# Jensen-Shannon divergence on one core: row groups in six rotating buffers, other column ranges, and the last row group closed on ScalarE

## The chip, the core and the metric

The kernel runs on one core of a Trainium2 chip. The time is the device time of one execution in microseconds (us), lower is better. The core's engines work side by side, each through its own instructions in order: TensorE (PE) multiplies matrices into PSUM, VectorE (DVE) does elementwise arithmetic and reductions, ScalarE (ACT) evaluates functions such as the logarithm, GpSimd (POOL) here only issues loads, SyncE (SP) issues loads and the store. Sixteen DMA engines move the data.

## The reference

```python
# p, q: (1024, 4096) fp32, each row sums to 1
m = 0.5 * (p + q)
kl_pm = np.sum(p * np.log(p / (m + 1e-8) + 1e-8), axis=-1)
kl_qm = np.sum(q * np.log(q / (m + 1e-8) + 1e-8), axis=-1)
return (0.5 * (kl_pm + kl_qm)).astype(np.float32)   # (1024,)
```

The kernel takes a logarithm of p, of q and of p+q for every column, so three logs for each column of a row: with a = ln p, b = ln q and c = ln((p+q)/2), the result is half the sum of p(a-c) + q(b-c). All three logs carry the same scale inside, which cancels.

## The kernel before

The 1024 rows are eight row groups of 128 rows, one row per partition, with 4096 columns each. Every row group is cut into column ranges, by four tables that need not agree: LOADS (what one DMA brings), LOGS (what one ScalarE instruction takes of p and q), SUMS (what PE adds up to p+q in one PSUM tile, and what one log of the sum takes), PRODUCTS (the width of a tile that holds the logs of p and q).

All input is loaded once. The first two ranges of row group 0 come as fp32 over the SyncE and ScalarE queues (lines 169 to 172). All others come through POOL's queue (lines 179 and 180, `cast_loads`), which casts fp32 to fp16 on the way: p and q of each range, 27 instructions each. Before the change every row group has an SBUF tile of its own (`data`, lines 155 to 158), so no load waits for a tile; all are issued in the order of the table.

The operations have one-letter names, with the number of their range:

- `a`: VectorE adds p and q of a range that came as fp32 (line 240). `F`: PE adds p and q of any other range by multiplying both with the identity into one PSUM tile, 512 columns at a time, p then q (line 265). Two PSUM tiles take turns.
- `p`, `q`: ScalarE logs p, then q, of one range of LOGS; from range SPLIT on, one instruction takes both (`q`, line 281). `c`: ScalarE logs a sum (line 299). There are C_BUFS tiles for c.
- `u`, `x` (row groups 0 to 5): VectorE subtracts c from both logs (line 311), then multiplies by p and q (line 321). `X`: PE adds the products up into the row group's PSUM accumulator of 256 columns (line 360, 256 columns a matmul).
- `m`, `s`, `M`, `S` (row groups 6 and 7, from APART on): the products p ln p, q ln q (line 328) and (p+q) c (line 339) are formed apart, which needs no subtraction, and PE adds them up with weights 0.5 and -0.5. The last FUSED_M of the m and the last FUSED_S of the s (lines 332 and 343) multiply and reduce in one VectorE instruction, into a running sum `run`.
- `f`: VectorE folds a row group's accumulator into one column of the result (line 382, or line 385 with the running sum). In the last row group ScalarE folds (`A`, line 371, Copy with an accumulated output) and VectorE adds the running sum (`f7`, line 376).
- `W`: PE multiplies without effect, to stay busy (line 253).

The order of each engine's operations is written out by hand in PE_ORDER, ACT_ORDER and DVE_ORDER. A loop at the end of the kernel emits them so that each operation comes after those it needs (`after`), without changing the order on an engine. The store of the result (line 470) is last.

The end of the three orders before:

```python
# ScalarE: ... c29 q27 q28 c30 q29 c31 q30 q31 q32 A7
# VectorE: ... s30 m26 s31 m27 m28 m29 f7
# TensorE: ... F30 F31 M24 M25 W10 M26 W4 M27 M28
```

Of the kernel before, what the change touches and what calls it, by code (L numbers as in the profile page):

```python
# [13 lines left out]
AW = 256  # L14
AB_BUFS = 5
C_BUFS = 4

LOADS = [  # L20
    [512, 256, 832, 960, 768, 768],
    [512, 896, 832, 768, 1088],
    [1280, 1408, 1408],
    [1152, 1408, 1536],
    [1280, 1536, 1280],
    [1408, 1408, 1280],
    [256, 1536, 1536, 768],
    [2048, 2048],
]
LOGS = [  # L30
    [512, 256, 832, 960, 768, 768],
    [512, 896, 832, 768, 1088],
    [1280, 1408, 1408],
    [1152, 1408, 1536],
    [1280, 1536, 1280],
    [1408, 1408, 1280],
    [256, 1536, 1536, 768],
    [768, 1024, 896, 512, 512, 384],
]
PRODUCTS = [  # L40
    [512, 256, 832, 1728, 768],
    [512, 896, 832, 1856],
    [1280, 1408, 1408],
    [1152, 1408, 1536],
    [1280, 1536, 1280],
    [1408, 1408, 1280],
    [1792, 1536, 768],
    [768, 1024, 896, 512, 512, 384],
]
SUMS = [  # L50
    [512, 256, 448, 384, 384, 384, 960, 768],
    [512, 896, 832, 768, 1088],
    [1280, 1408, 1408],
    [1152, 1408, 1536],
    [1280, 1536, 1280],
    [1408, 1408, 1280],
    [256, 1536, 1280, 1024],
    [1536, 1408, 1152],
]
HW = 2  # L60
SPLIT = 5

APART = 6
FUSED_M = 1
FUSED_S = 4

# [6 lines left out]
ACT_ORDER = """  # L73
p0 q0 c0 p1 q1 c1 p2 q2 c2 c3 p3 q3 c4 c5 p4 q4 c6 q5 c7 q6 c8 q7 c9 q8 c10 q9 c11 q10 c12
q11 c13 q12 c14 q13 c15 q14 c16 q15 c17 q16 c18 c19 q17 q18 c20 c21 q19 c22 q20 c23 q21
c24 c25 q22 c26 q23 q24 c27 q25 c28 q26 c29 q27 q28 c30 q29 c31 q30 q31 q32 A7
"""
PE_ORDER = """
W22 F2 F3 X0 X1 F4 F5 X2 X3 F6 X4 X5 F7 F8 X6 F9 X7 F10 X8 F11 X9 F12 X10 X11 F13 W8 X12
F14 F15 X13 F16 X14 F17 X15 F18 X16 F19 X17 F20 X18 F21 X19 F22 X20 F23 X21 F24 F25 X22  # L80
F26 S25 X23 F27 F28 S26 X24 M21 F29 S27 M22 M23 F30 F31 M24 M25 W10 M26 W4 M27 M28
"""
DVE_ORDER = """
a0 a1 u0 x0 u1 x1 u2 u3 x2 x3 u4 u5 x4 x5 u6 x6 u7 x7 u8 x8 f0 u9 x9 u10 x10 u11 x11 u12
x12 u13 f1 x13 u14 x14 u15 x15 u16 x16 f2 u17 x17 u18 x18 u19 x19 f3 u20 x20 u21 x21 u22
f4 x22 u23 s25 x23 u24 s26 x24 m21 s27 f5 m22 s28 m23 s29 m24 f6 m25 s30 m26 s31 m27 m28
m29 f7
"""
# [3 lines left out]
def kernel(  # L92
# [46 lines left out]

    small = ctx.enter_context(tc.tile_pool(name="small", bufs=1))  # L140
    lnp = ctx.enter_context(tc.tile_pool(name="lnp", bufs=AB_BUFS))
    mid = ctx.enter_context(tc.tile_pool(name="mid", bufs=C_BUFS))
# [9 lines left out]
    for i in range(HW):  # L152
        t32 = small.tile([P, 2, loads[i][2]], fp32, tag=f"pq32_{i}")
        early.append(t32)
    data = []
    for g in range(n_rg):
        t16 = small.tile([P, 2, n_cols - (split if g == 0 else 0)], fp16, tag=f"pq{g}")
        data.append(t16)

    def pq(g, c0, w):  # L160
        if g == 0:
            for i in range(HW):
                if loads[i] == (g, c0, w):
                    return early[i]
            c0 -= split
            assert c0 >= 0
        return data[g][:, :, c0 : c0 + w]
# [7 lines left out]
    nc.scalar.activation(out=warm, in_=warm, func=Act.Ln)  # L175
    def cast_loads(some):
        for g, c0, w in some:
            v = pq(g, c0, w)
            nc.gpsimd.dma_start(out=v[:, 0, :], in_=pv[g, :, c0 : c0 + w])  # L179
            nc.gpsimd.dma_start(out=v[:, 1, :], in_=qv[g, :, c0 : c0 + w])  # L180

    cast_loads(loads[HW : HW + 1])
    ident = small.tile([P, P], fp16, tag="ident")
# [4 lines left out]
    nc.vector.memset(zero, 0.0)  # L188
    cast_loads(loads[HW + 1 :])
    half = small.tile([P, P], fp16, tag="half")  # L190
# [24 lines left out]
    for g in range(n_rg):  # L215
        own = [o for o in dve_order if o == ("f", g) or (fused(*o) and range_of(*o)[0] == g)]
        if g < n_rg - 1 or act_folds:
            own = [o for o in own if o[0] != "f"] + [("f", g)]
        chain[g] = own
# [4 lines left out]
    def next_run(o, g):  # L224
        before = state["last"].get(g, 0.0)
        if o == chain[g][-1]:
            return before, res[:, g : g + 1]
        k = state["used"]
        state["used"] += 1
        state["last"][g] = run[:, k : k + 1]  # L230
        return before, run[:, k : k + 1]
# [92 lines left out]
    def op_m(k):  # L324
        g, c0, w = prods[k]
        u = pq(g, c0, w)
        if not fused("m", k):
            nc.vector.tensor_tensor(out=ab[k], in0=u, in1=ab[k], op=Alu.mult)  # L328
            product["M", k] = ab[k]
            return  # L330
        before, now = next_run(("m", k), g)
        nc.vector.tensor_tensor_reduce(
            out=ab[k], in0=u, in1=ab[k], scale=0.5, scalar=before,
            op0=Alu.mult, op1=Alu.add, accum_out=now,
        )

    def op_s(j):
        if not fused("s", j):
            nc.vector.tensor_tensor(out=c[j], in0=s[j], in1=c[j], op=Alu.mult)  # L339
            product["S", j] = c[j].unsqueeze(1)  # L340
            return
        before, now = next_run(("s", j), parts[j][0])
        nc.vector.tensor_tensor_reduce(  # L343
            out=c[j], in0=s[j], in1=c[j], scale=-0.5, scalar=before,
            op0=Alu.mult, op1=Alu.add, accum_out=now,
        )

    def add_up(kind, i):
# [9 lines left out]
        for n, (t, b) in enumerate(todo):  # L358
# [7 lines left out]
            )  # L366

    def op_A(g):
        folded = small.tile([P, 1], fp32, tag="folded")
        unused = small.tile([P, AW], fp16, tag="unused")  # L370
        nc.scalar.activation(out=unused, in_=acc[g][:, :AW], func=Act.Copy, accum_out=folded)  # L371
        state["folded"] = folded

    def op_f(g):
        if act_folds and g == n_rg - 1:
            nc.vector.tensor_tensor(
                out=res[:, g : g + 1], in0=state["folded"], in1=state["last"][g], op=Alu.add
            )
            return
        before, now = next_run(("f", g), g)  # L380
# [24 lines left out]
    def after(kind, i):  # L405
# [21 lines left out]
        if kind == "f":  # L427
            if act_folds and i == n_rg - 1:
                return chain[i][:-1] + [("A", i)]
            return chain[i][: chain[i].index(("f", i))] + adds[i]  # L430
        if kind == "A":
            return adds[i]
        return []

    accumulator(0)
    ops = dict(a=op_a, F=op_F, p=op_p, q=op_q, c=op_c, u=op_u, x=op_x, m=op_m, s=op_s, f=op_f, A=op_A)
    queues = [list(pe_order), list(act_order), list(dve_order)]
    emitted = set()
# [25 lines left out]
    if act_folds:  # L464
        want.add(("A", n_rg - 1))
    assert emitted == want
    pe_order = [o for o in pe_order if o[0] != "W"]
# [33 lines left out]
```

## Time and profile before

| | |
|---|---|
| median of 4 runs | 98.15 us (97.92 to 98.23) |
| profiled execution, its own time | 98.23 us |
| its span (first to last instruction) | 96.4 us |
| granted TensorE clock, mean | 0.982 |
| PE / DVE / ACT / POOL busy, share of the span | 74% / 85% / 93% / 30% |
| read from HBM | 33.55 MB, 348 GB/s over the span |

The profile is one execution. An engine's busy time is the time in which it worked on instructions; the span is cut into 40 equal slices of 2.41 us, and a digit gives the busy share of a slice in tenths. A wait is idle time of an engine, put down to whatever released it last. The chain that ended last is followed back from the last instruction, at each step to what released it. A row of the timeline has the start in us, the duration in us, the engine, the line, the operation, the output and inputs with their sizes, and in brackets the idle time just before it and who ended it. The trace also holds when each of the sixteen parts of a load landed; a load counts as landed with the last of them.

### The profile page before, as it was taken

What the parts mean: (1) busy time and instruction counts of PE and PEld (TensorE: products, weight loads), DVE (VectorE), ACT (ScalarE), POOL (GpSimd) and SP (SyncE); (2) the same over time, 40 slices, a digit from 0 to 9 for tenths busy, and PEclk for the clock granted to TensorE, in tenths of its full rate; (3) what the DMA queues carried; (4) which work ended last, traced back from release to release, by engine and by line L of the source; (5) the groups of instructions that cost most, each with busy time, mean ns of one, the idle gap of its engine ahead of it and who ended that gap; (6) DMA issues with size and microseconds to landing.
All of it is one profiled execution on the core that took longest, in us unless ns stands there. A gap on an engine that the chain in (4) does not pass through costs nothing.

```text
span 96.4 us, 1311 instructions
## 1 busy us (share of the span) xinstructions
PE 71.3 (74%) x468; PEld 45.7 (47%) x468; DVE 81.8 (85%) x87; ACT 89.7 (93%) x74; POOL 29.3 (30%) x60
## 2 busy tenths in 40 slices
PE   0799884976589659996785974984966979797740
PEld 0575441643456127662461642652643766566520
DVE  1289869999964989898979989979999999999990
ACT  3599999999979999999999999999999999999960
POOL 5974466453242424232332423235300000000000
PEclk9999999999999975999999999999999999999999
DMA  2999999999999999999999999999999999300000
GB/s 42 321 194 205 205 205 207 208 211 218 206 211 213 208 212 212 212 216 209 215 210 209 215 211 210 209 209 213 208 207 220 212 214 216 59 0 3 0 0 2
DMA packets 8502, 17.25 MB, mean 179 GB/s; under 512 B 1072, under 2 KB 3888, under 8 KB 8496
## 3 DMA queue, kind: packets, MB, share of 16 engines
q0 software_dynamic: 7776, 16.39, 89.6%
q1 hardware_dynamic: 432, 0.40, 1.5%
q10 hardware_dynamic: 288, 0.39, 1.2%
q8 instruction: 3, 0.05, 0.2%
q14 instruction: 3, 0.02, 0.1%
HBM read 33.55 MB, written 0.00 MB: 348 GB/s over the span
## 4 chain that ended last, share of the span: by engine, by line
ACT 39%; DMA 25%; issue 23%; DVE 6%; PE 2%; POOL 2%; ACTq 0%; POOLq 0%
DMA t<-in_q_dram 25%; ACT ab_t L281 23%; ACT c_t L299 15%; DVE c_t L339 2%; DVE c_t L343 1%; DVE ab_t L311 1%; PE acc_t L360 1%; PE st L265 1%; POOL t L179 1%; DVE ab_t L328 1%; POOL t L180 1%; ACT unused L371 0%; POOL ident masks.py:199 0%; POOL ident masks.py:197 0%; ACTq L299 0%
## 5 line engine op out<-in xcount | busy, mean ns | idle before, releaser
L281 ACT ACTIVATE ab_t<-t 128x2816 f16<-128x2816 f16 (+15 forms) x38 | 62.6, 1687 | 1.8 <-DMA t<-in_p_dram 1.1
L265 PE MATMUL st<-t,ident 128*128 128x512 f16 (+4 forms) x144 | 34.0, 357 | 7.4 <-DMA t<-in_q_dram 6.1
L360 PEld LDWEIGHTS <-half 128*128 128x128 f16 x268 | 25.7, 99 | 21.1 <-issue 16.7
L311 DVE TENSOR_TENSOR ab_t<-ab_t,c_t 128x2816 f16<-128x2816 f16 (+12 forms) x25 | 29.3, 1180 | 6.9 <-ACT c_t L299 6.1
L299 ACT ACTIVATE c_t<-st 128x1408 f16<-128x1408 f32 (+13 forms) x30 | 32.3, 1100 | 0.0
L360 PE MATMUL acc_t<-t,half 128*128 128x256 f16 (+2 forms) x200 | 24.8, 271 | 8.7 <-DVE t L321 8.4
L321 DVE TENSOR_TENSOR t<-t,ab_t 128x2816 f16<-128x2816 f16 (+11 forms) x23 | 28.2, 1234 | 1.2
L265 PEld LDWEIGHTS <-ident 128*128 128x128 f16 x144 | 13.7, 98 | 21.1 <-issue 10.8
L179 POOL DMA_DIRECT2D t<-in_p_dram x27 | 14.5, 536 | 20.2 <-DMA t<-in_p_dram 19.2
L180 POOL DMA_DIRECT2D t<-in_q_dram x27 | 14.3, 531 | 19.9 <-DMA t<-in_q_dram 19.7
L360 PE MATMUL acc_t<-ab_t,half 128*128 128x256 f16 x68 | 8.9, 270 | 3.0 <-DVE ab_t L328 2.9
L328 DVE TENSOR_TENSOR ab_t<-t,ab_t 128x1536 f16<-128x1536 f16 (+5 forms) x8 | 9.3, 1171 | 0.1
L253 PE MATMUL acc_t<-ones,ident 128*128 128x256 f16 x22 | 4.8, 414 | 3.1 <-POOL ident masks.py:199 3.1
L253 PEld LDWEIGHTS <-ident 128*128 128x128 f16 x22 | 3.2, 147 | 4.3 <-POOL ident masks.py:199 3.1
L339 DVE TENSOR_TENSOR c_t<-st,c_t 128x256 f16<-128x256 f32 (+2 forms) x3 | 3.6, 1217 | 0.0
L343 DVE CUSTOM_DVE_ANT_0 c_t<-st,c_t,run 128x1408 f16<-128x1408 f32 (+1 forms) x2 | 3.1, 1548 | 0.0
L343 DVE CUSTOM_DVE_ANT_0 c_t<-st,c_t 128x1024 f16<-128x1024 f32 (+1 forms) x2 | 3.0, 1483 | 0.0
L253 PE MATMUL acc_t<-ones,zero 128*128 128x256 f16 x22 | 2.9, 273 | 0.0
L175 ACT ACT_TABLE_LOAD x1 | 1.3, 1283 | 1.7 <-PEq L485 1.7
L382 DVE TENSOR_REDUCE res<-acc_t 128x1 f32<-128x256 f32 x6 | 2.5, 417 | 0.0
L253 PEld LDWEIGHTS <-zero 128*128 128x128 f16 x22 | 2.1, 98 | 0.2
L240 DVE TENSOR_TENSOR s<-t 128x512 f32<-128x512 f32 (+1 forms) x2 | 1.1, 558 | 1.2 <-DMA t<-in_q_dram 1.1
(24 smaller groups left out, 10.6 us busy)
## 6 DMA issues: line engine op xcount, KB each, us to landing
t<-in_p_dram POOLq DMA_DIRECT2D x5, 352.0 KB, 12.6
t<-in_q_dram POOLq DMA_DIRECT2D x5, 352.0 KB, 13.0
t<-in_p_dram POOLq DMA_DIRECT2D x4, 384.0 KB, 11.8
t<-in_q_dram POOLq DMA_DIRECT2D x4, 384.0 KB, 12.0
t<-in_p_dram POOLq DMA_DIRECT2D x4, 320.0 KB, 13.0
t<-in_q_dram POOLq DMA_DIRECT2D x4, 320.0 KB, 12.7
t<-in_p_dram POOLq DMA_DIRECT2D x2, 512.0 KB, 13.1
t<-in_q_dram POOLq DMA_DIRECT2D x2, 512.0 KB, 14.4
```

Source lines behind the costliest of these rows:

```text
L179: nc.gpsimd.dma_start(out=v[:, 0, :], in_=pv[g, :, c0 : c0 + w])
L180: nc.gpsimd.dma_start(out=v[:, 1, :], in_=qv[g, :, c0 : c0 + w])
L253: nc.tensor.matmul(out=acc[g][:, :AW], lhsT=weights, rhs=ones, start=alone, stop=alone)
L265: nc.tensor.matmul(out=st[:, b : b + m], lhsT=ident, rhs=v[:, t, b : b + m], start=t == 0, stop=t == 1,)
L281: nc.scalar.activation(out=ab[k][:, which, o : o + w], in_=pq(g, c0, w)[:, which, :], func=Act.Ln, bias=TINY, scale=SHIFT,)
L299: nc.scalar.activation(out=c_t[:, :w], in_=s[j], func=Act.Ln, bias=SHIFT * 1e-8, scale=SHIFT * 0.5)
L311: nc.vector.tensor_tensor(out=v, in0=v, in1=c[j].unsqueeze(1).to_broadcast([P, 2, parts[j][2]]), op=Alu.subtract,)
L321: nc.vector.tensor_tensor(out=into, in0=u, in1=v, op=Alu.mult)
L328: nc.vector.tensor_tensor(out=ab[k], in0=u, in1=ab[k], op=Alu.mult)
L339: nc.vector.tensor_tensor(out=c[j], in0=s[j], in1=c[j], op=Alu.mult)
L343: nc.vector.tensor_tensor_reduce(out=c[j], in0=s[j], in1=c[j], scale=-0.5, scalar=before, op0=Alu.mult, op1=Alu.add, accum_out=now,)
L360: nc.tensor.matmul(out=acc[g][:, :m], lhsT=less if kind == "S" else half, rhs=v[:, t, b : b + m], start=(kind, i) == adds[g][0] and n == 0 ...
```

## The change

- **Buffers.** The eight tiles of the row groups become a pool of six (`datap`, DATA_BUFS). A row group's loads are emitted as an operation `L`; those of row groups 6 and 7 come after the sums of row groups 0 and 1 are complete, and reuse their tiles. C_BUFS goes from 4 to 5.
- **Loads.** The two fp32 ranges become 576 and 384 columns (512 and 256 before). The number of loads stays: 4 fp32, 54 casting.
- **Ranges.** All four tables are new in most row groups, and with them the three written orders. Logs of p and q separate go up to range 7 (SPLIT), the last five s are fused (four before).
- **The end.** In row group 7 ScalarE's fold takes the running sum as its bias and writes the result itself: Identity in place of Copy. Since the bias is added at each of 256 columns, the fused m and s of that row group scale by 1/256 more (`share`). VectorE's `f7` is gone; `f6`, the fold of row group 6, moves to the end of VectorE's order.

In the new order POOL's instructions stand as before, loads in the order of the table; the first load of row groups 6 and of 7 each has a wait for PE, VectorE and ScalarE in addition.

```diff
-C_BUFS = 4
+C_BUFS = 5
+DATA_BUFS = 6
 LOADS = [
-    [512, 256, 832, 960, 768, 768],
-    [512, 896, 832, 768, 1088],
-    [1280, 1408, 1408],
+    [576, 384, 864, 1088, 1184],
+    [1280, 1536, 1280],
     [1152, 1408, 1536],
-    [1280, 1536, 1280],
-    [1408, 1408, 1280],
-    [256, 1536, 1536, 768],
+    [1024, 1024, 1024, 1024],
+    [1024, 1024, 1024, 1024],
+    [2048, 640, 128, 768, 512],
+    [1280, 1280, 1536],
     [2048, 2048],
 ]
 LOGS = [
-    [512, 256, 832, 960, 768, 768],
-    [512, 896, 832, 768, 1088],
-    [1280, 1408, 1408],
+    [576, 384, 864, 1088, 1184],
+    [1280, 1536, 1280],
     [1152, 1408, 1536],
-    [1280, 1536, 1280],
+    [2048, 2048],
+    [2048, 2048],
     [1408, 1408, 1280],
-    [256, 1536, 1536, 768],
-    [768, 1024, 896, 512, 512, 384],
+    [1280, 1280, 1536],
+    [1152, 1024, 768, 512, 256, 256, 128],
 ]
 PRODUCTS = [
-    [512, 256, 832, 1728, 768],
-    [512, 896, 832, 1856],
-    [1280, 1408, 1408],
+    [576, 384, 864, 1088, 1184],
+    [2816, 1280],
     [1152, 1408, 1536],
-    [1280, 1536, 1280],
-    [1408, 1408, 1280],
-    [1792, 1536, 768],
-    [768, 1024, 896, 512, 512, 384],
+    [2048, 2048],
+    [2048, 2048],
+    [2816, 1280],
+    [1280, 1280, 1536],
+    [1152, 1024, 768, 512, 256, 256, 128],
 ]
 SUMS = [
-    [512, 256, 448, 384, 384, 384, 960, 768],
-    [512, 896, 832, 768, 1088],
-    [1280, 1408, 1408],
+    [576, 384, 864, 768, 320, 1184],
+    [1280, 1536, 1280],
     [1152, 1408, 1536],
-    [1280, 1536, 1280],
+    [1024, 1024, 1024, 1024],
+    [1024, 1024, 1024, 1024],
     [1408, 1408, 1280],
-    [256, 1536, 1280, 1024],
-    [1536, 1408, 1152],
+    [1280, 1280, 1536],
+    [1536, 1408, 640, 512],
 ]
-SPLIT = 5
+SPLIT = 7
-FUSED_S = 4
+FUSED_S = 5
...
+p0 q0 c0 p1 q1 c1 p2 q2 c2 p3 q3 c3 c4 p4 q4 c5 p5 q5 c6 p6 q6 c7 q7 c8 q8 c9 q9 c10 q10
+c11 c12 q11 c13 c14 q12 c15 c16 q13 c17 c18 q14 c19 q15 c20 c21 q16 c22 q17 c23 q18 c24
+q19 c25 q20 c26 q21 c27 q22 c28 q23 c29 q24 q25 q26 q27 A7
...
+W22 F2 X0 X1 F3 F4 X2 F5 X3 X4 F6 X5 F7 X6 F8 F9 X7 F10 X8 X9 F11 F12 X10 F13 W8 F14 X11
+F15 X12 F16 X13 F17 X14 F18 X15 F19 X16 X17 F20 F21 X18 X19 F22 X20 F23 X21 F24 S23 F25
+X22 M16 F26 M17 S24 W6 F27 M18 F28 M19 F29 W4 M20 W4 M21 W3 M22 M23 M24
...
+a0 a1 u0 x0 u1 x1 u2 x2 u3 u4 x3 x4 u5 x5 u6 f0 x6 u7 x7 u8 x8 u9 x9 f1 u10 x10 u11 x11
+u12 u13 x12 x13 f2 u14 u15 x14 x15 u16 u17 x16 x17 f3 u18 u19 x18 x19 u20 f4 x20 u21 x21
+u22 s23 x22 m16 s24 m17 s25 f5 m18 s26 m19 s27 m20 s28 m21 s29 m22 m23 m24 m25 f6
...
+    datap = ctx.enter_context(tc.tile_pool(name="datap", bufs=DATA_BUFS))
...
+    def op_L(i):
+        g, c0, w = loads[i]
+        if g not in data:
+            t16 = datap.tile([P, 2, n_cols], fp16, tag="pq")
+            data[g] = t16
+        v = pq(g, c0, w)
+        nc.gpsimd.dma_start(out=v[:, 0, :], in_=pv[g, :, c0 : c0 + w])
+        nc.gpsimd.dma_start(out=v[:, 1, :], in_=qv[g, :, c0 : c0 + w])
...
-            out=ab[k], in0=u, in1=ab[k], scale=0.5, scalar=before,
+            out=ab[k], in0=u, in1=ab[k], scale=0.5 * share(g), scalar=before,
...
-            out=c[j], in0=s[j], in1=c[j], scale=-0.5, scalar=before,
+            out=c[j], in0=s[j], in1=c[j], scale=-0.5 * share(g), scalar=before,
...
+    def share(g):
+        return 1.0 / AW if act_folds and g == n_rg - 1 else 1.0
+
     def op_A(g):
-        folded = small.tile([P, 1], fp32, tag="folded")
         unused = small.tile([P, AW], fp16, tag="unused")
-        nc.scalar.activation(out=unused, in_=acc[g][:, :AW], func=Act.Copy, accum_out=folded)
-        state["folded"] = folded
+        before, now = next_run(("A", g), g)
+        nc.scalar.activation(
+            out=unused, in_=acc[g][:, :AW], func=Act.Identity, bias=before, accum_out=now
+        )
 
     def op_f(g):
-        if act_folds and g == n_rg - 1:
-            nc.vector.tensor_tensor(
-                out=res[:, g : g + 1], in0=state["folded"], in1=state["last"][g], op=Alu.add
-            )
-            return
...
         if kind == "A":
-            return adds[i]
+            return chain[i][:-1] + adds[i]
+        if kind == "L":
+            g = loads[i][0] - DATA_BUFS
+            return adds[g] if g >= 0 else []
...
+    load_order = [("L", i) for i in range(HW + 1, len(loads))]
+    queues = [load_order, list(pe_order), list(act_order), list(dve_order)]
```

## The prediction

> **What bounds the kernel now.** First the page: the busy times of the engines, then their slices.
>
> ```profile
> span 96.4 us, 1311 instructions
> ...
> PE 71.3 (74%) x468; PEld 45.7 (47%) x468; DVE 81.8 (85%) x87; ACT 89.7 (93%) x74; POOL 29.3 (30%) x60
> ...
> ACT  3599999999979999999999999999999999999960
> ...
> DMA  2999999999999999999999999999999999300000
> ```
>
> Two things are full: ScalarE from slice 3 to 38, and the DMA engines from slice 2 until about 84 us. The second row matters as much as the first. One column of p and q costs ScalarE three logs at 0.833 ns (below), 2.5 ns and overheads; it costs the load stream 2.42 ns (56.42 us for the 23,296 column pairs between the landings at 27.86 and 84.28). They run almost abreast, so each can stop the other. Next, what ScalarE waited for:
>
> ```profile
> ACT L175 <- PEq L485: 1.7, 1, 1.7
> ACT ab_t L281 <- DMA t<-in_p_dram: 1.1, 1, 1.1
> ACT unused L371 <- PE acc_t L360: 0.7, 1, 0.7
> ACT ab_t L281 <- DMA t<-in_q_dram: 0.7, 1, 0.7
> ```
>
> Between the first load and the last fold there is one named wait, 0.7 us for a load. The timeline has its place, and the stretch where the last loads are used:
>
> ```profile
> 27.95 2.34 ACT L281 ACTIVATE ab_t<-t 128x2560 f16<-128x2560 f16 x1 [0.70 <-DMA t<-in_q_dram]
> ...
> 83.94 2.33 PE L265 MATMUL st<-t,ident 128*128 128x512 f16 x12
> ...
> 86.00 1.46 ACT L299 ACTIVATE c_t<-st 128x1408 f16<-128x1408 f32 x1
> ...
> 93.42 0.38 ACT L371 ACTIVATE unused<-acc_t 128x256 f16<-128x256 f32 x1 [0.73 <-PE acc_t L360]
> ...
> 93.93 0.16 DVE L376 TENSOR_TENSOR res<-folded,run 128x1 f32<-128x1 f32 x1 [0.18 <-ACT unused L371]
> 94.12 0.35 SPq L470 DMA_DIRECT2D out_dram<-res  x1
> ```
>
> The last q load is issued at 69.12 us and takes 15.16 us (line 180's row gives 15.2 as its longest), so it lands at 84.28. The first six of the twelve matmuls at 83.94 form p+q of row group 7, columns 1536 to 2944 (F30): four steps of 0.216 us, one of 0.163 and a last matmul of 0.33, so they end at 85.30. ScalarE logs that sum (c30) at 86.00. The margin is 0.70 us. The result stands at 94.09; the span ends 2.34 later, and the execution's 98.23 us is 1.80 above its span. The median is 98.15, so 0.08 comes off at the end.
>
> **The change, part by part.**
>
> *ScalarE's own work.* Between back-to-back rows, a log out of SBUF takes 0.833 us per thousand values and 0.092 on top (2816 values, 41.70 to 44.14: 2.44; 1024 values, 89.82 to 90.77: 0.95); out of PSUM the addition is 0.06 (1408 values, end 44.25 to end 45.49: 1.23). All 98,304 values cost 81.92 in both kernels. Before there are 40 such instructions out of SBUF and 28 out of PSUM: 81.92+3.68+1.68 = 87.28. After there are 37 and 28: 87.00. That is 0.28 less, if ScalarE sets the end.
>
> *Loads.* The same bytes are read, by 4 fp32 loads and 54 casting ones in both kernels, in the same order of p and q. A load lands this long after the one before it, from the landing stamps: 256 columns 0.37 us, 512 0.65, 768 0.95, 960 1.18, 1088 1.31, 1152 1.39, 1280 1.56, 1408 1.71, 1536 1.85, 2048 2.46. Interpolated: 128 0.22, 640 0.80, 1024 1.25, 1184 1.43. The q of 832 columns lands at 7.58. The new one of 864 comes later by 384 more fp32 columns at 1.19 ns (0.46) and 64 casting ones (0.07): 8.11. The remaining loads of one tensor add up to 37.57, both to 75.14. Once, near 24 us, a landing slips: the p load of 1280 columns lands 2.43 us after its forerunner instead of 1.56, and the stream stays 0.86 late. With that the last load lands at 84.11; with one straight line through all widths instead of the rows, at 84.31. I take 84.2. The stream gains or loses nothing worth a tenth.
>
> What the slip is: the page's queue q8 has three instruction packets of 16 KB, and the stamps put the first at 23.71 us, 0.96 us long, on one DMA engine of 16. The Trainium skill (Runtime: NRT & Kernel Launch, section Instruction fetch mechanics) says engines refill in blocks of 16 KiB and calls the cost of a boundary mostly hidden. The stamps disagree: a load counts only when its slowest sixteenth is in. By the page's rule the last landing would be at 83.3 and the result 0.9 earlier.
>
> *Small loads.* The row of 256 columns says 0.37 us a load, so the 128-column pair adds 0.1 over its share. The Trainium skill (DMA: Bandwidth & Descriptors, section Measured) gives 0.95 us for 64 KB and advises 1 MiB; the pair would then cost 1.9 instead of 0.4 and the result come 1.5 later. The row decides: loads overlap here in a full queue.
>
> *The buffer rotation.* Row group 6's first load waits until row group 0's sum is complete (the first fold, at 19.83 us, shows when) and group 7's until group 1's (32.85). POOL issues them after about 57 us. Nine more loads queue behind the first wait, and all of row groups 6 and 7 behind them; none is held, so the cost is nothing. Were a buffer free only at 59 us or later, each microsecond of it would be one at the end.
>
> *The last loads' place.* Here the change costs. In the new ScalarE order c27 (the same columns 1536 to 2944) stands after only 1152 columns of the row group's p and q logs, before after 1792. That is 1280 values and one instruction earlier, 1.16 us less work ahead of it, against a margin of 0.70. So c27 waits for PE, which waits for the last load: 84.2, +0.03, then q's second matmul 0.216, p's and q's third 0.163 + 0.33: 84.94; c27 starts at 84.97 and ends at 86.29 (1.17 + 0.15 after a wait). The other side of this: without that wait ScalarE would be there at about 84.55 (4.45 for the start, 87.00 of work, 0.9 of waits, less 7.8 for c27 and what follows). The 0.9 comes from adding landings and logs in order: the q loads that end row group 1, the three of group 2 and the second of group 3 land at 23.5, 27.1, 30.5, 34.2 and 39.3, and ScalarE reaches them 0.1, 0.3, 0.4, 0.03 and 0.1 earlier. (The logs of 4096 values in groups 3 and 4 each wait for two loads of a tensor, which is in this.) So c27 waits some 0.4, and the early waits drop out of the sum: only the last landing counts.
>
> *From c27 to the end.* 2048 values 1.80, 640 0.59, 1536 1.37, 512 0.49, 1024 0.95, 512 0.52 twice, 256 0.31: 6.55, so the last log ends at 92.84. VectorE's fused product of 768 values took 1.02; at 1.04 ns a value the one of 256 takes 0.49 and ends near 93.41. In parallel the last plain product is added by PE until about 93.43. The fold then takes 0.38 + 0.09 (93.42 to 93.90 before): 93.93. It now carries the running sum as bias; a bias column from SBUF is shown by no row of a fold, so it may cost between -0.05 (row noise) and 0.19 (its accumulator-read row); I take 0, since every log already has one. The closing addition (0.16 + 0.18 of waiting) goes. The fold of group 6 (f6, 0.48) moves behind the last product, 93.33 to 93.81, beside the ScalarE fold: free.
>
> *Elsewhere, hidden.* VectorE's fp32 product covers 192 columns more (384 values, 0.2 us) where VectorE has 0.3 to 0.7 idle; one more fused sum costs 0.01; PE issues 461 matmuls for 468. PE has idle 8.7 us before line 360. If VectorE were late here, ScalarE would meet it only through five c buffers.
>
> **Sum.** 93.93 against 94.09: 0.16 less; 98.07 against 98.23, or 97.99 beside the median.
>
> **Rivals.**
> 1. *An earlier stream*: the packet that slips falls on a DMA engine that is not the last. For: the second and third packets, at 48.5 and 74.8, moved no last landing. Against: the wait at 27.95 carries the slip, and the four runs lie within 0.31 us. Price: 0.86 off, 97.1; faster from a landing before 84.07.
> 2. *The stream runs dry, slower*: place, row group 5's five short loads. From the ninth on, a casting load is issued when the eighth before it has landed (landing 32.95, issue 33.24). When group 6's first is issued, the queue holds 640q, 128, 768 and 512: 4.5 us. The first load of the kernel needed 4.9 from issue to landing, 1.0 of it its own transfer: 3.9. It fits by 0.6; were pickup 1.4 longer, the stream would lose 0.8 and the result come at 98.8. A second slip on the same engine costs the same. Slower from a landing after 84.65.
> 3. *The loads do not matter*: ScalarE's 0.28 and the closing 0.2 to 0.3 are gained in full: 97.6. Against: the margin above.
> 4. *Nothing moves*, because the bound stays the wait near 28 us with equal waits later: 98.1, inside the forecast.
>
> **How the numbers follow.** About 0.3% (0.29 us) can be told from no change. Forecast, 97.7 to 98.3, 4 included: 0.60, of which 0.40 lies within 0.3%, 0.16 below and 0.04 above. Rival 1 0.12 and rival 3 0.08, both faster. Rival 2 0.15, slower. The last 0.05 go to PE: its clock stood at 0.83 between 34 and 44 us, and such a stretch under F27 costs about 0.5, slower, though part may fall within. Faster 0.36, same 0.42, slower 0.22. The range takes rival 1's inner half and rival 2: 97.2 to 98.8.
>
> **What will show it.** Right: ScalarE waits for PE's sums at c27 (about 0.4 us near 84.6), the last load lands at 84.2, f6 ends before the fold. Wrong: c27 without a wait; a last landing away from 84.2 by more than 0.3; idle DMA slices near 60 us; a fold longer than 0.5 us.

## The result, and the profile after

| | before | after |
|---|---|---|
| median | 98.12 us (56 runs, 97.58 to 99.07) | 97.86 us (35 runs, 97.63 to 99.25) |
| ratio, 95% interval | | 0.997 (0.9959 to 0.9981) |
| profiled execution, span | 98.23, 96.4 | 97.83, 96.1 |
| last load landed | 84.28 | 83.83 |
| ScalarE's fold starts, result stands | 93.42, 94.09 | 93.16, 93.72 |

The change saves 0.26 us of 98.12. The interval leaves out 1, but the gain is as small as the 0.29 us that the prediction named as the least that can be told from no change. The forecast was 98.0. Ratios leave out slow executions, of the changed kernel the two at 99.12 and 99.25 us.

First the page of the changed kernel:

```profile
span 96.1 us, 1290 instructions
...
PE 68.6 (71%) x461; PEld 44.5 (46%) x461; DVE 81.0 (84%) x84; ACT 89.6 (93%) x69; POOL 29.3 (31%) x60
...
ACT  3499999999999999999999999999999999989970
...
DMA  2999999999999999999999999999999999300000
GB/s 44 367 212 212 210 214 212 206 216 212 207 211 217 206 206 212 209 209 210 208 212 212 217 206 198 206 214 207 216 212 216 212 215 217 63 0 0 0 0 2
```

The busy shares stand nearly as before (PE 71% for 74%). What differs is where ScalarE's idle time lies. Its waits (total us, times, longest), then its timeline:

```profile
ACT L172 <- PEq L489: 1.7, 1, 1.7
ACT ab_t L282 <- DMA t<-in_p_dram: 1.4, 1, 1.4
ACT unused L377 <- PE acc_t L362: 0.7, 1, 0.7
ACT c_t L300 <- PE st L266: 0.3, 1, 0.3
```

```profile
82.23 2.12 ACT L282 ACTIVATE ab_t<-t 128x2304 f16<-128x2304 f16 x1
84.62 1.34 ACT L300 ACTIVATE c_t<-st 128x1408 f16<-128x1408 f32 x1 [0.27 <-PE st L266]
...
90.09 2.40 ACT L282 ACTIVATE ab_t<-t 128x1024 f16<-128x1024 f16 x4
93.16 0.47 ACT L377 ACTIVATE unused<-acc_t,run 128x256 f16<-128x256 f32 x1 [0.66 <-PE acc_t L362]
93.53 0.19 ACT L377 ACTIVATION_READ_ACCUMULATOR unused<-acc_t,run 128x1 f32 x1
```

The 0.7 us for a load near 28 us is gone. In its place c27, the log of the sum of the last loads' columns, waits for PE. The first log starts at 4.53 here, in before at 4.22; that is scatter of the first landings, since other profiles with these loads have 4.09 to 4.38. The last logs end at 92.49 (before 92.69). From there to the result it is 1.23 us, before 1.40. The chain that ended last (start, duration) shows what c27 hangs on:

```profile
67.33 16.50 DMA t<-in_q_dram
83.83 0.04 issue
83.88 0.71 PE st L266 x3
84.59 0.02 issue
84.62 0.04 ACT c_t L300
```

The last load lands at 83.83, PE adds its columns in 0.71, and ScalarE starts at once. Over the whole span the same chain gives DMA 65% and ScalarE 8%; in before it gave ScalarE 39% and DMA 25%. In these two executions the end has moved from ScalarE to the loads.

### The profile page after: what moved, and what is told of

Its sections match the earlier page's. It is cut to its first block, busy times and chain, and to the rows that moved or that the text cites. A ratio compares the mean times of both kernels' runs of the same rounds, so it can differ in the third digit from the quotient of the medians.

```text
span 96.1 us, 1290 instructions
## 1 busy us (share of the span) xinstructions
PE 68.6 (71%) x461; PEld 44.5 (46%) x461; DVE 81.0 (84%) x84; ACT 89.6 (93%) x69; POOL 29.3 (31%) x60
## 4 chain that ended last, share of the span: by engine, by line
DMA 65%; issue 11%; ACT 8%; DVE 8%; PE 3%; POOL 1%; DVEq 0%; ACTq 0%; POOLq 0%
DMA t<-in_q_dram 60%; ACT ab_t L282 6%; DMA t<-in_p_dram 6%; DVE ab_t L312 2%; DVE t L322 2%; PE st L266 2%; DVE c_t L345 2%; DVE ab_t L329 1%; ACT c_t L300 1%; PE acc_t L362 1%; POOL t L180 1%; ACT unused L377 0%; DVEq L500 0%; ACTq L500 0%; DVEq L322 0%
## 5 line engine op out<-in xcount | busy, mean ns | idle before, releaser
L282 ACT ACTIVATE ab_t<-t 128x2560 f16<-128x2560 f16 (+15 forms) x35 | 61.1, 1777 | 1.4 <-DMA t<-in_p_dram 1.4
L266 PE MATMUL st<-t,ident 128*128 128x512 f16 (+6 forms) x138 | 32.5, 357 | 5.7 <-DMA t<-in_q_dram 5.0
L312 DVE TENSOR_TENSOR ab_t<-ab_t,c_t 128x2048 f16<-128x2048 f16 (+10 forms) x23 | 28.8, 1269 | 6.9 <-ACT c_t L300 4.1
L362 PE MATMUL acc_t<-t,half 128*128 128x256 f16 (+1 forms) x192 | 23.4, 268 | 13.5 <-DVE t L322 13.3
L300 ACT ACTIVATE c_t<-st 128x1024 f16<-128x1024 f32 (+10 forms) x28 | 30.9, 1131 | 0.3 <-PE st L266 0.3
L322 DVE TENSOR_TENSOR t<-t,ab_t 128x2048 f16<-128x2048 f16 (+8 forms) x21 | 27.4, 1326 | 0.6
L362 PE MATMUL acc_t<-ab_t,half 128*128 128x256 f16 (+2 forms) x74 | 9.2, 267 | 1.6 <-DVE ab_t L322 1.0
L329 DVE TENSOR_TENSOR ab_t<-t,ab_t 128x2560 f16<-128x2560 f16 (+6 forms) x9 | 9.6, 1087 | 0.4 <-ACT ab_t L282 0.2
L345 DVE CUSTOM_DVE_ANT_0 c_t<-st,c_t,run 128x1408 f16<-128x1408 f32 (+2 forms) x3 | 3.3, 1103 | 0.3 <-ACT c_t L300 0.3
L345 DVE CUSTOM_DVE_ANT_0 c_t<-st,c_t 128x1536 f16<-128x1536 f32 x2 | 3.5, 1750 | 0.0
```

The source lines that it names most:

```text
L266: nc.tensor.matmul(out=st[:, b : b + m], lhsT=ident, rhs=v[:, t, b : b + m], start=t == 0, stop=t == 1,)
L282: nc.scalar.activation(out=ab[k][:, which, o : o + w], in_=pq(g, c0, w)[:, which, :], func=Act.Ln, bias=TINY, scale=SHIFT,)
L300: nc.scalar.activation(out=c_t[:, :w], in_=s[j], func=Act.Ln, bias=SHIFT * 1e-8, scale=SHIFT * 0.5)
L312: nc.vector.tensor_tensor(out=v, in0=v, in1=c[j].unsqueeze(1).to_broadcast([P, 2, parts[j][2]]), op=Alu.subtract,)
L322: nc.vector.tensor_tensor(out=into, in0=u, in1=v, op=Alu.mult)
L345: nc.vector.tensor_tensor_reduce(out=c[j], in0=s[j], in1=c[j], scale=-0.5 * share(g), scalar=before, op0=Alu.mult, op1=Alu.add, accum_out=now,
```

## The experiments

Two theories stood against each other.

- **Theory A.** The changed kernel's end is pinned to its last landing, through PE's sum and c27. Before's end hangs on ScalarE's own work, with the last loads there in time (margin about 0.7 us). The new fold pays only where the running sum is ready when PE's accumulator is, which the narrow last ranges bring.
- **Rival.** The last loads have slack in both kernels, and the gain is ScalarE's fewer instructions, the fold, or both.

Ratios below are to before on the same chip; the changed kernel's, 0.997, is that of the result above. The landing stamps of the profiled executions are gathered after the runs.

**One more load pair, in both kernels.** An unread pair of 256 columns ahead of the last pair:

```diff
+        if i == len(loads) - 1:
+            spare = small.tile([P, 2, 256], fp16, tag="spare")
+            nc.gpsimd.dma_start(out=spare[:, 0, :], in_=pv[g, :, 0:256])
+            nc.gpsimd.dma_start(out=spare[:, 1, :], in_=qv[g, :, 0:256])
```

> The changed kernel, with one more pair of loads of 256 columns, into a tile that nobody reads, ahead of the last pair. Theory A (the last load sets the end, through F27 and c27): a pair of 256 columns took 0.37 us a load in the trace of before, so the last load lands 0.74 later, c27 starts 0.74 later, and the time is 97.86 + 0.74 = 98.6. Rival (ScalarE's and VectorE's own work sets the end, and c27's wait of 0.4 is cover for something else that is late anyway): at most 0.3 more, 97.9 to 98.1.

> The kernel before, with the same extra pair of 256 columns ahead of its last pair. Theory A: here F30 ended 0.70 us before ScalarE came to c30, so 0.74 more of load time eats the margin and costs 0.05 to 0.1: 98.2. If the load stream set the end of this kernel too, it would be 98.12 + 0.74 = 98.9.

Measured: the changed kernel 98.57 (ratio 1.0058, 1.0028 to 1.0087), before 98.30 (1.0027, 1.0001 to 1.0054). The same pair costs one kernel 0.9% and the other 0.3%. ScalarE's timeline of the changed kernel with the pair, then of before with it:

```profile
86.02 1.34 ACT L304 ACTIVATE c_t<-st 128x1408 f16<-128x1408 f32 x1 [1.28 <-PE st L270]
```

```profile
85.99 1.46 ACT L303 ACTIVATE c_t<-st 128x1408 f16<-128x1408 f32 x1
```

The bracket is the difference. In the changed kernel the wait for PE grows from 0.27 to 1.28. (Not all of that is the load, which lands 0.65 later, at 84.48: in that execution the granted PE clock stood at 0.50 from 80.3 to 83.7 us, and PE, busy without a break, came to these sums late. So the profile shows more than the 0.7 us by which the medians differ, or the 0.9 of the ratios. The nine executions with a mean granted clock of 0.99 or more have a median of 98.53, so the cost does not come from the clock.) In before the last load lands 0.71 later than without the pair, at 84.99, and the log of its sum starts where it did (86.00 without). Theory A holds for the landing: in before's profile it had slack, in the changed kernel's it has none. Before's median still rises by 0.3%, more than the 0.05 to 0.1 us expected and barely clear of noise; its profile does not show where.

**The sums one range later.** If c27 is too early in ScalarE's order, moving it should win the wait back:

```diff
-... q20 c26 q21 c27 q22 c28 q23 c29 q24 q25 ...      (ScalarE)
+... q20 q21 c26 q22 c27 q23 c28 q24 c29 q25 ...
-... m18 s26 m19 s27 m20 s28 m21 s29 m22 ...          (VectorE)
+... m18 m19 s26 m20 s27 m21 s28 m22 s29 ...
-... F29 W4 M20 W4 M21 W3 M22 M23 M24                 (TensorE)
+... F29 M20 M21 M22 M23 M24
```

> The changed kernel, where ScalarE logs the sums of row group 7 one place later (q21 c26 q22 c27 q23 c28 q24 c29), VectorE's products of them move accordingly, and PE's 11 idle matmuls after F29 are left out, since F29 comes later and they would hold up the last products. Theory A: ScalarE's two waits (0.19 at c26, 0.38 at c27) vanish, its last log ends at 91.9 instead of 92.5, and VectorE, which then has more left, ends 0.3 earlier than now: 97.5 to 97.6. Rival (the wait at c27 is cover): no difference, 97.8 to 97.9. If PE's clock falls for want of the idle matmuls, its last sums cost some 0.1 to 0.3 of that.

Measured: 97.74 (0.9967, 0.9942 to 0.9992), between the two and not to be told from the change as it is. ScalarE waits for no sum any more; VectorE is late instead. Its timeline in the change as it is, then with the later sums, then the fold's row:

```profile
85.99 1.69 DVE L345 CUSTOM_DVE_ANT_0 c_t<-st,c_t,run 128x1408 f16<-128x1408 f32 x1 [0.26 <-ACT c_t L300]
...
92.58 0.48 DVE L333 CUSTOM_DVE_ANT_0 ab_t<-t,ab_t,run 128x256 f16<-128x256 f16 x1
```

```profile
87.25 1.68 DVE L345 CUSTOM_DVE_ANT_0 c_t<-st,c_t,run 128x1408 f16<-128x1408 f32 x1
...
92.48 0.48 DVE L333 CUSTOM_DVE_ANT_0 ab_t<-t,ab_t,run 128x256 f16<-128x256 f16 x1
```

```profile
93.06 0.47 ACT L377 ACTIVATE unused<-acc_t,run 128x256 f16<-128x256 f32 x1 [1.11 <-PE acc_t L362]
```

The product of c27 comes 1.26 later than in the change as it is, the last fused product 0.10 earlier. ScalarE's last logs end at 91.96, half a us earlier, and the fold then idles 1.11 instead of 0.66. So c27's wait, though it is on the path, is worth some 0.1: VectorE stands right behind ScalarE.

**Before with the new end alone.** Identity fold with the running sum as bias, weights shared, f6 last, no closing addition; loads and ranges of before:

```diff
-            out=unused, in_=acc[g][:, :AW], func=Act.Copy, accum_out=folded
+            out=unused, in_=acc[g][:, :AW], func=Act.Identity, bias=before, accum_out=now
...
-... s29 m24 f6 m25 s30 m26 s31 m27 m28 m29 f7
+... s29 m24 m25 s30 m26 s31 m27 m28 m29 f6
```

> The kernel before with only the new end: the fold of row group 7 takes the running sum as bias (Identity), and the fold of row group 6 stands last on VectorE. Loads, ranges and the other orders are those of before. Theory A: the bias makes the fold wait for the fused product of 768 values, which ends at 93.75 in the trace of before, so the fold starts at 93.79 instead of 93.42, takes 0.57, and the result stands at 94.35 instead of 94.09: 0.26 slower, 98.4. Rival (the gain of the change is the closing addition that goes): the addition and its wait, 0.16 and 0.18, are saved, 97.8 to 97.9.

Measured: 98.66 (1.0049, 1.002 to 1.0078): slower than before. (Its profiled execution, 98.13, is its fastest: the last logs end at 92.30, 0.39 earlier than in before's profile, and the fold still starts no earlier, at 93.46. The row below shows the wait, the ratio what it costs.)

**The changed kernel with 384 columns in its last range**, as before had (the last two of 256 and 128 put together):

```diff
-    [1152, 1024, 768, 512, 256, 256, 128],
+    [1152, 1024, 768, 512, 256, 384],
```

> The changed kernel with the last two ranges of row group 7's logs and products, 256 and 128 columns, made one of 384, as wide as the last one of before. Theory A: ScalarE saves one log's 0.09, but the fused product after the last log has 768 values instead of 256, 1.02 us instead of 0.49, and the fold with its bias waits for it: last log at 92.4, product until 93.5, fold 0.57: the result at 94.05 instead of 93.72, 98.15 to 98.2. Rival (the end is set by PE's sums, which wait for the same logs): within 0.1 of 97.86.

Measured: 98.29 (1.0007, 0.9988 to 1.0026): the gain is gone. Both show the same wait. First the row of before with the new end, then the fold's row in the timeline of the changed kernel with the last range of 384:

```profile
ACT unused L377 <- DVE run L333: 1.2, 1, 1.2
```

```profile
93.66 0.47 ACT L377 ACTIVATE unused<-acc_t,run 128x256 f16<-128x256 f32 x1 [1.15 <-DVE run L333]
```

The releaser is now `run`, not PE's `acc_t`: the fold takes the running sum as its bias and has to wait for VectorE's last fused product, 768 values wide here and 256 in the change. The narrow last ranges are a condition of the new end, worth about 0.4 us.

**The changed kernel with the old fold.** Copy into `folded`, and VectorE adds the running sum after m25 and f6:

```diff
-            out=unused, in_=acc[g][:, :AW], func=Act.Identity, bias=before, accum_out=now
+            out=unused, in_=acc[g][:, :AW], func=Act.Copy, accum_out=folded
...
-... m22 m23 m24 m25 f6
+... m22 m23 m24 m25 f6 f7
```

> The changed kernel with the old end: Copy fold, then VectorE adds the running sum (m25 f6 f7), nothing else altered. In the profile of after the result stood 0.56 us after the fold's start (93.16 to 93.72), in that of before 0.67 (93.42 to 94.09). Theory A (in after's narrow last ranges the running sum is in time, so the bias fold saves the closing addition and nothing else): 0.1 us slower than after, 97.95 to 98.0. Rival (the bias makes the fold wait for the running sum as much as the addition cost): 97.8 to 97.86, no slower than after.

Measured: 97.92 (0.9968, 0.9949 to 0.9988). The medians cannot tell it from the change. In the profile the fold and the addition are:

```profile
93.49 0.38 ACT L376 ACTIVATE unused<-acc_t 128x256 f16<-128x256 f32 x1 [0.63 <-PE acc_t L361]
```

```profile
94.00 0.16 DVE L381 TENSOR_TENSOR res<-folded,run 128x1 f32<-128x1 f32 x1 [0.17 <-ACT unused L376]
```

From the fold's start the result takes 0.67 us here, 0.56 with Identity: Identity with the bias takes 0.09 more than Copy (0.47 against 0.38; function and bias were not changed apart), and the addition it replaces takes 0.20. So the new fold saves 0.1 at best; whether it does in the median stays open.

**f6 ahead of the last products.**

```diff
-... s28 m21 s29 m22 m23 m24 m25 f6
+... s28 f6 m21 s29 m22 m23 m24 m25
```

> The changed kernel with the fold of row group 6 (0.48 us on VectorE) ahead of m21 instead of at the end. Theory A (VectorE is as late as ScalarE over the last ten us, so 0.48 us put among its last products comes out at the end, less what idle it finds there): fold 0.2 to 0.3 later, 98.1. Rival (VectorE has slack there, and f6's new place is worth nothing): 97.85.

Measured: 98.17 (0.9996, 0.9972 to 1.0021), 0.26% above the change's ratio, as Theory A has it; the intervals touch. VectorE's f6, then the fold:

```profile
89.99 0.48 DVE L387 CUSTOM_DVE_ANT_0 junk<-acc_t,ones,run 128x256 f16<-128x256 f32 x1
```

```profile
93.79 0.47 ACT L377 ACTIVATE unused<-acc_t,run 128x256 f16<-128x256 f32 x1 [1.04 <-PE acc_t L362]
```

The fold's idle time grows from 0.66 to 1.04: 0.38 of VectorE's 0.48 comes out at the end.

**The first fp32 ranges back at 512 and 256 columns**, the next at 1056; alone, and together with three loads in row group 5 (next experiment):

```diff
-    [576, 384, 864, 1088, 1184],
+    [512, 256, 1056, 1088, 1184],
```

> The changed kernel with the fp32 loads of before, 512 and 256 columns, and a third range of 1056 in place of 864. ScalarE's first log then starts near 4.2 us instead of 4.53. Theory A (the load stream sets the end): in the two traces the first casting pair is complete at 7.58 us after 3200 columns (1536 of them fp32) and at 7.72 after 3648 (1920 fp32), so fp32 columns cost next to nothing there; with 448 of them cast instead, at 1.16 to 1.2 ns, the last load lands 0.4 to 0.5 later: 98.25 to 98.35. Rival (ScalarE's early start counts): 0.3 less, 97.55.

> The changed kernel with row group 5 in three loads and the first two fp32 ranges back at 512 and 256 columns. With the five loads of row group 5 the small first ranges measured 98.31, in a profile whose PE clock was 0.50 from 13 to 16 us. If the small first ranges cost by themselves (q2 waits 0.7 to 0.8 us for the first casting pair, and ScalarE never gets the lead that it has in after): 0.2 to 0.4 above the three loads alone, 97.8 to 98.05, in runs at full clock too. If the halved clock of that profile, or the thin queue near 60 us, was the cause: 97.6 at full clock.

Measured: 98.31 (1.0013, 0.9984 to 1.0042) and 98.45 (1.0021, 0.9989 to 1.0052). The first time the number was Theory A's, but the profiled execution came to it by another path. Its last load landed at 83.77, as in the change. PE's clock stood at 0.50 from 12.6 to 16.0 us, ScalarE waited for PE there, and from then on it was so late that c27 found its sum ready:

```profile
16.44 1.16 ACT L300 ACTIVATE c_t<-st 128x1184 f16<-128x1184 f32 x1 [1.19 <-PE st L266]
...
84.97 1.51 ACT L300 ACTIVATE c_t<-st 128x1408 f16<-128x1408 f32 x1
```

The second has no such stretch in its profiled execution, and is 0.7% above the three loads alone. The half clock is a rival for the whole effect: four of the first's twelve executions and five of the second's have a mean granted clock below 0.99. The others have medians of 98.07 and 98.29, each against before on its chip still about 0.3% and 0.6% above the same kernel without the edit. So the small ranges cost by themselves, and the clock adds to it. The second's row of GB/s begins with a slower second slice than the change's (322 against 367):

```profile
GB/s 57 322 186 197 210 207 214 211 207 218 206 213 213 208 209 208 210 209 211 209 211 212 214 210 211 210 212 209 214 213 212 216 217 214 44 0 3 0 0 2
```

Its first casting pair has landed at 7.98, with three loads alone at 7.56. The 0.42 is near the 192 columns of each of p and q that the casting queue now has to bring, at 1.2 ns a column (0.46). The other profiles agree: with the small ranges alone the pair has landed at 8.02; with the change's first ranges at 7.49 to 7.72 in eight profiles and at 7.96 in one; with before's, whose pair has 64 casting columns less, at 7.46 to 7.58 in three. So the bigger fp32 loads took next to no time from the casting queue. ScalarE waits for the pair, and for loads later; c27's wait is as long as with three loads alone (0.26) and comes 0.68 later:

```profile
8.00 1.08 ACT L282 ACTIVATE ab_t<-t 128x1056 f16<-128x1056 f16 x1 [0.16 <-DMA t<-in_q_dram]
...
30.81 2.55 ACT L282 ACTIVATE ab_t<-t 128x2816 f16<-128x2816 f16 x1 [0.32 <-DMA t<-in_q_dram]
...
85.09 1.34 ACT L300 ACTIVATE c_t<-st 128x1408 f16<-128x1408 f32 x1 [0.29 <-PE st L266]
```

The last load lands at 84.31 instead of 83.63 (0.42 and another 0.26 of slips on the way). At 0.3 to 0.7 us this is, beside the narrow last ranges, the largest single part of the change that was found.

**Row group 5 in three loads, or in eight.** The short loads of row group 5 are where a rival of the prediction saw the stream run dry:

```diff
-    [2048, 640, 128, 768, 512],
+    [1408, 1408, 1280],                          (three)
+    [2048, 512, 256, 128, 128, 256, 256, 512],   (eight)
```

> The changed kernel with row group 5 loaded as three ranges of 1408, 1408 and 1280 instead of 2048, 640, 128, 768 and 512: the same bytes, two pairs of loads fewer. Theory A: the stream is never dry in either, and four loads at 0.07 us of fixed cost fewer bring the last load 0.27 earlier. c27 then waits 0.1 instead of 0.4, but VectorE, which ended only 0.1 earlier when that wait was taken away by another order, gives back a part: 97.6 to 97.8. If the short loads had let the stream run dry in the changed kernel: 97.3 or less. If fixed costs are hidden: 97.86, no difference.

> The changed kernel with row group 5 loaded as 2048, 512, 256, 128, 128, 256, 256 and 512 columns: the same bytes, three pairs of loads more. The load that follows eight short ones is issued when the queue holds the rest of them. My reckoning: three pairs add 0.4 us of fixed cost; and with 2.9 us from an issue to its first packet (POOL's first load in both traces) and eight in flight, the queue is empty for 1.7 to 2.7 us in all. Theory A, with the stream running dry: 2.1 to 3.1 slower, 100.0 to 101.0. Rival (a pickup hidden however short the loads are): 0.4 slower, 98.3.

Measured: three 97.62 (0.9947, 0.9927 to 0.9966), eight 102.01 (1.037, 1.0333 to 1.0408). With eight the stream does run dry. Windows of that kernel, then of the change (busy time of each engine, clock, DMA share, GB/s):

```profile
60.00:65.00 5.00, 4.11 (x27) 2.49 (x26) 5.00 (x5) 5.00 (x4) 4.87 (x10) 1.00 0.92 112
65.00:70.00 5.00, 2.27 (x17) 1.41 (x15) 4.79 (x5) 4.97 (x3) 2.54 (x5) 1.00 0.95 150
```

```profile
60.00:65.00 5.00, 4.11 (x28) 2.52 (x27) 5.00 (x6) 5.00 (x4) 4.03 (x8) 1.00 1.17 210
65.00:70.00 5.00, 2.78 (x21) 1.82 (x20) 4.79 (x4) 5.00 (x4) 1.25 (x3) 1.00 1.09 211
```

From the ninth on a casting load is issued only when the eighth before it has landed (in the change landing 58.76, issue 59.05), and the stamps put the shortest time from issue to landing at 2.3 us, the loads of 128 columns mostly 0.18 apart: eight short loads do not cover their own latency. In the change the tightest load (q of 512 columns, issued 59.05) still lands 4.93 later with no gap behind it; with three loads none of those after 32 us takes less than 9.7. The price of eight is about 4 us over the change (ratios 1.037 and 0.997), where 2 to 3 had been reckoned. The profiled execution took 104.18, longer than any other of this kernel, and PE's clock stood at 0.50 in it from 70.8 to 77.7 and from 84.5 to 87.9 us, so how much of the price is the stream alone stays open. Three loads have the lowest ratio that was measured.

**Three loads and the later sums together.**

> The changed kernel with row group 5 in three loads and with the last row group's sums logged one range later, together. Alone they measured 97.62 and 97.74. If VectorE, which was the late engine with the later sums (c27's product at 87.25, fold waiting 1.11 us), sets the end, the earlier landing of 0.2 us brings little: 97.55 to 97.75, no better than the three loads alone. If the two gains are independent (landing and order): 97.4 to 97.5.

Measured: 97.77 (0.9952, 0.993 to 0.9973), no better than three loads alone. The two gains do not add up: with the later sums VectorE is the late engine (fold idle 1.10), and an earlier landing has nothing to release.

The landing stamps of the profiled executions, with the start of ScalarE's fold:

| kernel | last load landed | fold starts | between |
|---|---|---|---|
| change as it is | 83.83 | 93.16 | 9.33 |
| three loads | 83.63 | 92.96 | 9.33 |
| three loads, small fp32 ranges | 84.31 | 93.63 | 9.32 |
| old fold | 84.20 | 93.49 | 9.29 |
| f6 early | 84.09 | 93.79 | 9.70 |
| last range of 384 | 83.94 | 93.66 | 9.72 |
| sums later | 83.94 | 93.06 | 9.12 |
| three loads, sums later | 83.76 | 93.32 | 9.56 |
| change, one more pair | 84.48 | 94.57 | 10.09 |
| small fp32 ranges alone | 83.77 | 93.67 | 9.90 |
| eight loads | 89.49 | 99.50 | 10.01 |
| before, new end | 84.40 | 93.46 | 9.06 |
| before | 84.28 | 93.42 | 9.14 |
| before, one more pair | 84.99 | 93.40 | 8.41 |

In the first four the fold follows the last landing by 9.3 us, whatever the landing. In the last two it does not follow it at all. Between are the edits after which VectorE sets the end, earlier or later, and three executions (one more pair, small fp32 ranges alone, eight loads) in which PE's clock stood at 0.50 for a time and c27 started 1.2 to 1.5 us after the last landing instead of 0.8.

The landing itself scatters: in the five profiles with the change's own loads (the first of the table, old fold, f6 early, last range of 384, sums later) it lies between 83.83 and 84.20, in the two with three loads and its first ranges at 83.63 and 83.76.

## Why the prediction was right, and where it was not

- **What bounds before, and what takes its place: right.** Before had slack of about 0.7 at its last load (a later landing of 0.71 did not move the log of its sum). In the change c27 waits for PE's sum of the last load: predicted from 84.97 after a wait of about 0.4, measured from 84.62, which is 0.38 later than back-to-back rows would give; 0.27 of it shows as idle.
- **Loads: the step that was mis-sized.** "The new one of 864 comes later by 384 more fp32 columns at 1.19 ns (0.46)": they cost about 0.1 or less. The first casting pair had landed at 7.72, not 8.11; the 0.07 for 64 casting columns and scatter account for the 0.14 over before's 7.58. With smaller fp32 ranges it lands at 7.98 and 8.02. So "the stream gains or loses nothing worth a tenth" was wrong at its start by 0.4: 192 columns of each tensor leave the casting queue and come over the two other queues while its first load is still under way (landing 6.70). In the profiled execution the rest went as reckoned: 76.11 from that pair to the last landing, against 75.14 and a slip of 0.86, 76.00. That execution's landing of 83.83 is 0.37 from the 84.2, which the prediction listed as a sign of being wrong, and it lies before the 84.07 from which rival 1 counted the result as faster. In the four other profiles with the same loads the rest took 76.4 to 76.5, so that the start, too late by 0.4 to 0.6, and the rest, too short by 0.4 to 0.5, nearly cancel and the last load lands at 83.94 to 84.20. That 84.2 is near these is luck.
- **The slip.** In the change one p load of 1152 columns lands 2.32 after its forerunner instead of 1.39, near 24 us as before, and the next makes up 0.3. A second falls near 77.5, where q of 2048 takes 3.20 and the load after it 1.81 instead of 2.46. The queue's instruction packets stand at 23.5, 50.9 and 77.5. So the slips go with two of three packets, in this trace as in before's with one, against the "mostly hidden" of the Trainium skill (Runtime: NRT & Kernel Launch, section Instruction fetch mechanics). Over all 14 profiles, the step after the first packet is 0.6 to 1.2 longer than the median of its width in 13. With eight loads the third packet stands at 82.2 and the long step ends at 84.55. But in four variants of the change (f6 early, last range of 384, small fp32 ranges alone, three loads with the later sums) the packet near 78 is followed by no long step. That the packets cause the slips is argued, not shown.
- **ScalarE's own work: the count was off.** Before has 30 logs out of PSUM, not 28, so the change saves 0.40 and not 0.28. The sum did not use it, since the last landing ends the forecast's path; it would have made the rival that counts on ScalarE alone 0.12 faster.
- **From c27 on: right, shifted.** 6.55 was predicted to the last log; it ended at 92.49, 7.87 after c27's start, and the prediction's 92.84 was 7.87 after its own.
- **The fold: inside its bounds, not at the value taken.** Identity with the bias column takes 0.09 more (bounds -0.05 to 0.19, taken 0). The reason for the 0 does not hold: the logs' bias is a constant in the kernel, and their rows read `t` or a sum alone, where the fold's reads `run`. The fold starts at 93.16 (predicted 93.46) and the result stands at 93.72 (93.93).
- **f6 beside the fold: right.** Moved back among the products it costs about 0.3. What the prediction missed is how much of the end hangs on VectorE: its idle there was called cover, yet the narrow ranges, f6's place and the order of the sums each decide 0.1 to 0.4 through it.
- **The buffer rotation: right, it costs nothing.** Row group 6's first load is issued at 60.10, 0.55 after the eighth before it has landed; POOL idles 0.53 before it, and 0.45 before row group 7's first at 63.90. The stream does not notice: the first of them lands 1.52 after its forerunner, where other loads of 1280 columns take 1.55.
- **PE's clock.** The 0.83 between 34 and 44 us in before is a mean: the trace has 0.50 from 34.9 to 38.3 us and 1.00 around it.
- **Early waits: right in kind.** By the gaps between its rows ScalarE waits 0.02 to 0.17 at three loads between 30 and 39 us, and the wait near 28 us is gone.
- **Rivals.** The stream running dry did not happen, but it exists, and the change stands close to it. "The loads do not matter" fell with the extra pair. The earlier stream came, though by less than its price, and for another reason than the one given: not a lost slip but fp32 columns that cost next to nothing.

In sum the result stands 0.37 earlier in the profile than in before's, where 0.16 was forecast: the landing comes 0.37 earlier than 84.2, less the fold's 0.09 and 0.07 of small shifts. That the medians differ by 0.26 and the two profiled executions by 0.40 is within the scatter of before. So the path was right, and the nearness of the number rests on errors that partly cancel.

What stays open: whether the bias fold is worth its 0.1, and how much of the three loads' 0.2 over the change is real; the intervals of both touch the change's. The fifth c buffer and the new ranges of the middle row groups were not tried alone.

## What to carry to other kernels

When two resources run abreast, move each of them alone by a known amount (an extra unread load, an order shifted by one) before crediting an edit: the same pair of loads cost one kernel 0.9% and the other 0.3%. Bytes that another queue fetched while the main queue was still starting cost next to nothing here (384 columns, 0.1 us or less), and took 0.4 us off the start of the stream that sets the end. An operation that takes a running value as its operand inherits the lateness of the engine that makes it, so such a fusion needs a narrow last tile on that engine.

## What the hardware showed that was not expected

- 384 more fp32 columns over the SyncE and ScalarE queues in the first 5 us delayed the casting queue's first pair by about 0.1 us or less (7.49 to 7.72 in eight of nine profiles, 7.46 to 7.58 in before's three); the same columns in the casting queue cost 0.4 (7.98 and 8.02).
- In a full casting queue loads of 128 columns land 0.18 to 0.25 us apart, but from issue to landing none took less than 2.3. A row of them, with eight in flight, cut the stream from 210 to 112 GB/s.
- An Identity with a bias column took 0.47 us for 256 values where Copy took 0.38.
- A single profiled execution may carry a stretch in which PE's granted clock is 0.50, at a place that changes (12.6 to 16.0 us in one kernel, 80.3 to 83.7 in another); here it hid the cause of one result until a second kernel had the same edit without it. The five stretches in the 14 traces last 3.41 us, one of them twice that. Cut into windows of 3.41 us from where the clock first reaches 1.00, the traces have five windows at full clock in which PE was busy 38 to 44% of the time, and each is followed by half clock; in the 338 others PE was busy 45% or more, and none is. The longest idle gap in the five is 2.1 us.
